# Feed-forwards with five plain units, residual sums kept in the matmul banks by ScalarE, normalised activations made by ScalarE and GpSimd, and gate sums ahead of a weight split

## The chip, the cores and the metric

The kernel runs on one core of a Trainium2 chip. A core has five engines that run their own instruction queues in order and meet through semaphores: TensorE (PE, matmuls; its weight loads are listed apart as PEld), VectorE (DVE), ScalarE (ACT), GpSimd (POOL) and SyncE (SP, which issues the transfers between the main memory and the on-chip memory SBUF). Matmul results go into banks of an accumulation memory (PSUM) of 128 partitions x 512 float32 each. The metric is the time on the device of one execution, in microseconds, as the median of several runs.

## The reference, cut to what matters

A decoder trunk of two layers, one sequence of 512 tokens, width 1024. The even layer's attention has two kinds of heads, the odd layer's forgets. Each layer adds an attention part and a gated feed-forward to x. The change lies in the feed-forward, and in a few lines of layer 1's attention.

```python
def conv_glu_ffn(h, w_in, conv_w, conv_b, w_out):
    a, b = jnp.split(h @ w_in, 2, axis=-1)              # 1024 -> 2 x 2816
    taps = conv_w[:, None, :]
    a = lax.conv_general_dilated(a, taps, window_strides=(1,), padding=[(CONV_WIDTH - 1, 0)],
                                 dimension_numbers=('NWC', 'WIO', 'NWC'),
                                 feature_group_count=a.shape[-1]) + conv_b
    return (jax.nn.silu(a) * b) @ w_out                 # 2816 -> 1024

def reference(x, ...):
    for layer in range(DEPTH):
        h = rmsnorm(x, attn_norm[layer])
        ...
        x = x + conv_glu_ffn(rmsnorm(x, ffn_norm[layer]), ffn_w_in[layer], ffn_conv_w[layer],
                             ffn_conv_b[layer], ffn_w_out[layer])
    return rmsnorm(x, final_norm)
```

In layer 1, `log_f = log_sigmoid(f + b_f)` is a gate for each head and token, and its running sum over the tokens goes into the attention scores.

## The kernel before, in words

**Layout.** Activations lie transposed, features on the partitions: `X[0..7]` are eight tiles of 128 features x 512 tokens. Every float32 matmul operand is split into a high and a low part (`whi`/`wlo` for weights, `xh`/`xl` for activations, `gh`/`gl` for the gated middle), and each product is three matmuls: high by high, low by high, high by low. ScalarE makes high parts (a cast), VectorE low parts (a subtraction).

**The plan.** From the attention on, work is written as jobs with an engine, a cost, what they depend on, a priority (smaller is sooner) and the buffers they take and give back (class `Plan`). `Plan.run` places the jobs by their costs, engine by engine, and the kernel issues the instructions in that order; each engine then runs its own in program order. So a cost or a priority in a call of `add` sets an order, not a time.

**A feed-forward** (`ffn`) has 22 units of 128 columns of `a` and 128 of `b`. Each unit is conv, silu, product, and gives `gh[c]`, `gl[c]`. Two kinds of units:

- *Plain* (`plain`, the first `PLAIN` = 6): two half units, each 8 x 3 matmuls of 512 columns into one of two banks (`mm`). The activation that enters is x times the norm's weight, without the root; VectorE multiplies the bank by `rstd` afterwards (`fa`, `fb`).
- *Seven products* (`seven`, the other 16): a 2 x 2 block scheme that needs seven block products in place of eight. Each product is 4 x 3 matmuls of 256 columns. It works on sums of weight blocks (`total` on VectorE, `cross` on GpSimd, tiles `sr`, `sp`, split into `sxh`, `sxl`) and on sums of normalised activation blocks. Those are made once, by `sums(k)` for k = 0 to 3, while the plain units run: two normalised tiles (`gh<-x,ng,rstd`), four sums of half a tile (tiles `d1`, `d3`, named `gl` in the trace), and their high and low parts in the tiles `b1`, `b2`, `t1`, `t3`. The results of a unit are put together from the banks `t`, `o` and four `f` banks.

`gate` and `gated` finish a unit: a scaled copy and a silu on ScalarE (tile `tt`), two taps of the convolution (`tap`), the product and the low part on VectorE.

**The output projection** is done in four parts (`PARTS`), after 6, 12, 17 and 22 units. `out(m, p)` multiplies part p's units into output tile m: its weights (`wo`) are loaded and split, each of its 5 or 6 units is a step of three matmuls into an `mm` bank, and VectorE adds the bank to `X[m]` (`x<-x,mm`). On TensorE a seven-product unit has priority 100 + c and a step of `out` 200 + p, so the steps fill the places where a unit isn't ready. In the last layer the fourth part is done token by token and goes straight into the final norm (`tokens`).

**Loads.** All weights are issued by SP in one chain: `wraw` (512 KB, two buffers) for plain units and for one half of a seven-product unit, `wb` (512 KB, two buffers) for its other half, `wo` for the output.

**Layer 1's gate sums.** At the start of layer 1's attention the kernel runs a queue of generators (`fl`): one unit, a group of values that also gives `lf` (the log of the gate), and three more units. `cums` then casts `lf` and multiplies it with a triangle of ones. The weights of the unit `U[1]` are split on VectorE at about the same place (line 91 is the helper through which every operation is recorded, so all rows of the profile have that line).

Of the kernel before, what the change touches and what calls it, by code (L numbers as in the profile page):

```python
# [18 lines left out]
P = 128  # L19
# [3 lines left out]
NF = 22  # L23
# [15 lines left out]
PARTS = ((0, 6), (6, 12), (12, 17), (17, 22))  # L39
PLAIN = 6  # L40
# [143 lines left out]
def trunk(ctx, tc, A):  # L184
# [112 lines left out]
    def unit(src, use, ps=None, hl=None):  # L297

        h, l = weights(src, [P, NK, P]) if hl is None else hl
# [108 lines left out]
    class Mixer:  # L408
# [11 lines left out]
        def weights(self, src, shape, place=None, token="w", split=None):  # L420
# [9 lines left out]
            def hi():  # L430
# [5 lines left out]
                              b, prio=p, give=("wraw",))  # L436
# [709 lines left out]
    def ffn(layer, nl, final):  # L1146
# [7 lines left out]
        with ExitStack() as es:  # L1154
# [3 lines left out]
            plan = Plan(dict(PE=0.0, ACT=2.6, DVE=2.6, POOL=4.9, SP=-5.0), dict(PE=0.03), wraw=2, wb=2, wo=2, w=2, mm=2, f=4, t=1, o=1,  # L1158
                        a=2, tt=1, b=2, g=10, sr=2, sp=1, slot=NK, sq=2)
            plan.bufs["w"], plan.bufs["slot"] = [], []  # L1160
            add = plan.add
            M = Mixer(plan, None, None)
            GH, GL, GJ = {}, {}, {}
            B = {n: [fp.tile([P, H, w], F32R, tag=f"{n}{x}", bufs=1, name=f"{n}{x}") for x in "hl"]
                 for n, w in (("b1", W), ("b2", SEQ), ("t1", SEQ), ("t3", SEQ))}

            MV = dict(b11=("b1", LO), b21=("b2", LO), b22=("b2", HI), t1=("t1", LO), t2=("t1", HI), t3=("t3", LO), t4=("t3", HI))
# [4 lines left out]

            def split(h, l, x, n, prio, *deps, take=(), give=()):

                j = add("ACT", 0.19 + 0.00085 * n, lambda: act.copy(h(), x()), *deps, prio=prio, take=take)
                return add("DVE", 0.16 + 0.00104 * n, lambda: dve.tensor_sub(l(), x(), h().bitcast(F32)), j, prio=prio, give=give)

            def gate(c, box, *deps):
# [12 lines left out]
                j = add("DVE", 0.72, lambda: tap(2), j, prio=p)  # L1191
                j = add("DVE", 0.72, lambda: tap(1), j, prio=p, give=("a",))
                return add("ACT", 0.68, lambda: silu.append(act.activation(box["t"], box["t"], AF.Silu).ins), j, prio=p)

            def gated(c, box, *deps):
# [7 lines left out]
                GJ[c] = add("DVE", 0.69, lambda: dve.tensor_sub(GL[c], box["b"], GH[c].bitcast(F32)), j, prio=p, give=("b",))  # L1203
# [27 lines left out]
            def plain(c, root):  # L1231
                box = {}
                ps = []
                for u in range(2):
                    w = M.weights(A["wfi"][layer, 2 * c + u], [P, NK, P]) if c else (dict(h=first[u][0], l=first[u][1]), None)
                    lastu = (c, u) == (PLAIN - 1, 1)
                    bx, j = {}, None
                    for k in range(NK):
                        def step(k=k, w=w, bx=bx):
                            if k == 0:  # L1240
                                bx["ps"] = mm_bank()
# [5 lines left out]
                        j = add("PE", 0.685, step, w[1], j, prio=100 + c, take=("mm",) if k == 0 else (), give=give)  # L1247
# [11 lines left out]
                j = add("DVE", 0.69, fa, ps[0][1], root[0], prio=1, take=("a",), give=("mm",))  # L1259
                t = gate(c, box, j)  # L1260
                j = add("DVE", 0.69, fb, ps[1][1], prio=1, take=("b",), give=("mm",))
# [3 lines left out]
            def sums(k, root):  # L1265

                x = {}

                def norm(c):
                    x[c] = g_tile("gh", F32)  # L1270
                    dve.scalar_tensor_tensor(x[c], X[c], ng[:, nl - 1, c:c + 1], rstd, op0=ALU.mult, op1=ALU.mult)
                    if c >= H:
                        x["d1"], x["d3"] = g_tile("gl", F32), g_tile("gl", F32)
                p = 2 + 0.1 * k
                j = add("DVE", 0.75, lambda: norm(k), root[0], prio=p, take=("g",))
                j = add("DVE", 0.75, lambda: norm(k + H), j, prio=p, take=("g",))
                eng, e, cost = (pool, "POOL", 0.74) if True else (dve, "DVE", 0.42)
                s1 = add(e, cost, lambda: eng.tensor_sub(x["d1"][:, LO], x[k][:, LO], x[k][:, HI]), j, prio=p)
                s2 = add(e, cost, lambda: eng.tensor_add(x["d1"][:, HI], x[k + H][:, HI], x["d1"][:, LO]), s1, prio=p)
                s3 = add(e, cost, lambda: eng.tensor_sub(x["d3"][:, LO], x[k + H][:, HI], x[k][:, HI]), s2, prio=p)  # L1280
                s4 = add(e, cost, lambda: eng.tensor_sub(x["d3"][:, HI], x["d1"][:, HI], x[k + H][:, LO]), s3, prio=p)
                part = lambda n, i: (lambda: B[n][i][:, k])
                a = split(part("b1", 0), part("b1", 1), lambda: x[k][:, LO], W, p, j, s4)
                b = split(part("b2", 0), part("b2", 1), lambda: x[k + H], SEQ, p, j, s4, give=("g",))
                c = split(part("t1", 0), part("t1", 1), lambda: x["d1"], SEQ, p, s2, s4)
                d = split(part("t3", 0), part("t3", 1), lambda: x["d3"], SEQ, p, s4, c, b, give=("g",))
                TJ.extend((a, b, c, d))

            order = [None] * 3
            count = [0]  # L1290

            def seven(c):

                w, box, sm, sj = [None] * 4, {}, {}, {}
                n0 = c * 0.001

                def load(u, pool_, tag):
# [555 lines left out]
```

## Time and profile before

| | |
|---|---|
| median of 3 runs | 1216.3 us (1215.74 to 1216.44) |
| the profiled execution | 1216.55 us |
| its span, first to last instruction | 1214.8 us |
| first feed-forward, first to last matmul of its own, about | 271 to 621 us |
| second feed-forward, about | 855 us to the end |
| granted TensorE clock | 0.999 |
| moved from the main memory | 119.80 MB, 100 GB/s over the span |

A row of a group reads: engine, operation, tiles written <- tiles read, shapes, count, then busy us and mean ns of one, then the engine's idle time just before and who ended it. A row of the order of time starts with the start and the duration in us. Matmuls overlap, so a matmul's duration (0.39 us for 512 columns) is longer than the distance from one start to the next; that distance is TensorE's pace. `mm<-xh,wlo` is a matmul of a plain unit, `mm<-gh,whi` one of `out`, and matmuls with `sxh` or `sxl` are those of seven-product units (named by their bank `f`, `t` or `o`).

### The profile page before, as it was taken

To read this page: it belongs to the slowest core of one execution; us is meant where nothing else is said; L and a number is where in the kernel's file an instruction comes from. 1 tells how busy PE (TensorE), PEld (TensorE's weight loads), DVE (VectorE), ACT (ScalarE), POOL (GpSimd) and SP (SyncE) were. 2 spreads that over 40 slices of the span, in tenths; PEclk is the share of its full clock that TensorE was granted. 3 is DMA by queue.
4 is the path that set the end of the run, shared out by engine and by line. 5 is a ranking of instruction groups with operands and counts; after the bars stand their busy time and mean duration, and the time that the engine had idled before them with its cause. 6 is when DMAs were issued, how large, how long until landed. Compare 5 with 4: busy or idle time off the path is not lost.

```text
span 1214.8 us, 19529 instructions
## 1 busy us (share of the span) xinstructions
PE 1205.3 (99%) x7491; PEld 1038.3 (85%) x7491; DVE 910.4 (75%) x1565; ACT 647.9 (53%) x1211; POOL 221.2 (18%) x262
## 2 busy tenths in 40 slices
PE   9999999999999999999999999999999999999998
PEld 6887877778898999999887878877889999999996
DVE  6867887679996898878774463446899779887883
ACT  6666577745554454444553664644555445454453
POOL 0000035423400100100121552411341000110100
PEclk9999999999999999999999999999999999999999
DMA  7322231122423223213224552322233223222331
GB/s 236 121 75 93 73 112 37 36 70 87 155 77 116 96 96 120 93 68 131 78 97 149 161 175 83 112 70 87 88 107 137 74 102 126 85 98 82 132 105 70
DMA packets 50685, 124.71 MB, mean 103 GB/s; under 512 B 6096, under 2 KB 16080, under 8 KB 50592
## 3 DMA queue, kind: packets, MB, share of 16 engines
q1 hardware_dynamic: 50304, 123.18, 30.3%
q8 instruction: 59, 0.97, 0.3%
q14 instruction: 34, 0.28, 0.1%
q10 hardware_dynamic: 288, 0.28, 0.1%
HBM read 119.80 MB, written 2.13 MB: 100 GB/s over the span
## 4 chain that ended last, share of the span: by engine, by line
PE 95%; DVE 2%; ACT 1%; issue 0%; POOL 0%; DMA 0%; DVEq 0%; SPq 0%; POOLq 0%; ACTq 0%
PE mm L91 55%; PE f L91 17%; PE t L91 12%; PE o L91 7%; PE s L91 4%; POOL e L91 0%; DMA x<-x 0%; DVE wlo L91 0%; ACT e L91 0%; DVE sxl L91 0%; DVE xl L91 0%; ACT whi L91 0%; DVE e L91 0%; DVE q L91 0%; ACT sq L91 0%
## 5 line engine op out<-in xcount | busy, mean ns | idle before, releaser
L91 PE MATMUL mm<-xh,whi 128*128 128x512 f32 x424 | 169.0, 399 | 0.0
L91 PE MATMUL mm<-xh,wlo 128*128 128x512 f32 x424 | 165.7, 391 | 0.0
L91 PE MATMUL mm<-xl,whi 128*128 128x512 f32 x424 | 165.3, 390 | 0.0
L91 DVE TENSOR_TENSOR wlo<-wraw,whi 128x1024 fp32r<-128x1024 f32 (+2 forms) x83 | 100.6, 1212 | 45.3 <-ACT whi L91 45.3
L91 POOL TENSOR_TENSOR sp<-wraw,wb 128x512 f32<-128x512 f32 x32 | 47.1, 1473 | 441.3 <-DMA wraw<-wfi 243.2
L91 PE MATMUL mm<-gh,wlo 128*128 128x512 f32 x312 | 122.1, 391 | 0.0
L91 PE MATMUL mm<-gh,whi 128*128 128x512 f32 x312 | 122.1, 391 | 0.0
L91 PE MATMUL mm<-gl,whi 128*128 128x512 f32 x312 | 121.4, 389 | 0.0
L91 ACT CAST whi<-wraw 128x1024 fp32r<-128x1024 f32 (+2 forms) x83 | 81.8, 985 | 65.3 <-PE mm L91 41.4
L91 DVE TENSOR_TENSOR x<-x,mm 128x512 f32<-128x512 f32 x96 | 65.4, 684 | 50.9 <-PE mm L91 50.5
L91 POOL TENSOR_SCALAR e<-e,dn 128x128 f32<-128x128 f32 (+3 forms) x128 | 76.5, 622 | 133.8 <-DVE dn L91 121.3
L91 PEld LDWEIGHTS mm<-xh,whi 128*128 128x128 f32 x424 | 79.8, 188 | 19.4 <-issue 3.7
L91 DVE SCALAR_TENSOR_TENSOR tt<-a,conv,tt 128x510 f32<-128x510 f32 x88 | 72.1, 819 | 31.5 <-ACT tt L91 30.7
L91 PEld LDWEIGHTS mm<-xh,wlo 128*128 128x128 f32 x424 | 79.8, 188 | 17.2 <-DVE wlo L91 1.9
L91 PEld LDWEIGHTS mm<-xl,whi 128*128 128x128 f32 x424 | 79.6, 188 | 16.8
L91 ACT CAST sxh<-sr 128x512 fp32r<-128x512 f32 x96 | 56.4, 617 | 68.1 <-DVE sr L91 68.1
L91 ACT ACTIVATE e<-e,nm 128x256 f32<-128x256 f32 (+3 forms) x128 | 70.8, 556 | 31.0 <-DVE nm L91 30.8
L91 ACT COPY a<-f 128x256 f32<-128x256 f32 x64 | 23.9, 373 | 112.6 <-PE f L91 111.7
L91 ACT CAST whi<-wo 128x768 fp32r<-128x768 f32 (+1 forms) x56 | 44.0, 789 | 54.4 <-PE mm L91 48.5
L91 PE MATMUL f<-t3l,sxh 128*128 128x256 f32 x256 | 72.4, 283 | 0.0
L91 PE MATMUL f<-t3h,sxl 128*128 128x256 f32 x256 | 72.4, 283 | 0.0
L91 PE MATMUL f<-t3h,sxh 128*128 128x256 f32 x256 | 72.4, 283 | 0.0
(311 smaller groups left out, 3496.1 us busy)
## 6 DMA issues: line engine op xcount, KB each, us to landing
wraw<-wfi SPq DMA_DIRECT2D x56, 512.0 KB
wb<-wfi SPq DMA_DIRECT2D x32, 512.0 KB
wraw<-wu SPq DMA_DIRECT2D x30, 512.0 KB
wo<-wfo SPq DMA_DIRECT2D x32, 384.0 KB
wraw<-wo SPq DMA_DIRECT2D x16, 512.0 KB
wo<-wfo SPq DMA_DIRECT2D x24, 320.0 KB
wraw<-wv SPq DMA_DIRECT2D x10, 512.0 KB
x<-x SPq DMA_DIRECT2D x16, 256.0 KB
```

Source lines behind the costliest of these rows:

```text
L91: r = f(*a, **k)
```

## The change

1. `PARTS` becomes ((0, 5), (5, 11), (11, 17), (17, 22)) and `PLAIN` 5: unit 5 is a seven-product unit, and the first output part has five units.
2. `sums(k)` is rewritten. ScalarE makes x times the norm's weight, GpSimd multiplies by `rstd`, in place, and makes the sums: one instruction of 128x512 for two differences, two of 128x256. All seven blocks of a k lie side by side, so that one cast (128x1792) and one low part (128x1792) do for all. The even k work in a tile `sx`, the odd ones in the tile `WB`, which is both buffers of the wide weights `wb`; the first wide load waits for the last low part. The priorities move these jobs among the plain units' splits.
3. `out(m, p)`, except for the first two tiles of the first part and for the part that feeds the next layer, starts from a bank into which ScalarE has copied `X[m]`, and ScalarE copies the bank back at the end; VectorE's addition goes.
4. On TensorE, units and output tiles have one common order (`at`), and a table of counts places the units between the tiles (`HOLD`). The last step of the first output tile is done after most of the second tile.
5. The low parts of plain units' weights get priority 1.05 (were 1.2), those of the first two output tiles too; some costs change.
6. In layer 1 the split of `U[1]`'s weights is issued behind the instruction that makes `lf`, and the gate sums come one step earlier.

The core of the diff:

```diff
-PARTS = ((0, 6), (6, 12), (12, 17), (17, 22))
-PLAIN = 6
+PARTS = ((0, 5), (5, 11), (11, 17), (17, 22))
+HOLD = 2
+PLAIN = 5
...
             c = self.plan.add("DVE", 0.16 + 0.00104 * n, lambda: dve.tensor_sub(box["l"], box["w"], box["h"].bitcast(F32)),
-                              b, prio=p, give=("wraw",))
+                              b, prio=p if low is None else low, give=("wraw",))
...
-                j = add("DVE", 0.72, lambda: tap(2), j, prio=p)
+                j = add("DVE", 1.0 if c < PLAIN else 0.77, lambda: tap(2), j, prio=p)
...
             def sums(k, root):
...
+                def weighted(c):
+                    out, src, _ = halves(c)
+                    act.activation(out, src, AF.Copy, scale=ng[:, nl - 1, c:c + 1])
+
+                def rooted(c):
+                    out, _, r = halves(c)
+                    pool.tensor_mul(out, out, r)
+                p = 1.2 + 0.0001 * (25,45,65,85)[k]
+                own = ("sx",) if n == 0 else ("wb", "wb")
+                if k in range(4):
+                    a = add("ACT", 0.62, lambda: weighted(k), prio=p, take=own)
+                    b = add("ACT", 0.62, lambda: weighted(k + H), a, prio=p)
+                    j = add("POOL", 1.9, lambda: rooted(k), a, root[0], prio=p)
+                    j = add("POOL", 1.9, lambda: rooted(k + H), b, j, prio=p)
...
+                j = add("POOL", 1.48, lambda: pool.tensor_sub(two(4, 6), two(1, 3), hi.unsqueeze(1).to_broadcast([P, 2, W])), j, prio=p)
+                j = add("POOL", 1.1, lambda: pool.tensor_add(e1, hi2, d1), j, prio=p)
+                j = add("POOL", 1.1, lambda: pool.tensor_sub(e3, e1, lo2), j, prio=p, lat=3.0)
+                j = add("ACT", 0.19 + 0.00085 * NC, lambda: act.copy(BX[0][:, k], x[:, W:]), j, prio=p + 0.004)
+                TJ.append(add("DVE", 2.6, lambda: dve.tensor_sub(BX[1][:, k], x[:, W:], BX[0][:, k].bitcast(F32)), j, prio=p + 0.004,
+                              give=("sx",) if n == 0 else ("wb", "wb")))
...
+                def wide_load(j):
+                    return add("SP", 0.35, load(1, "wb"), j, TJ[-1], prio=1 + n0, take=("wb",), lat=3.3)
...
+                if c == PLAIN:
+                    la = raw_load(M.prev_load)
+                    lb = M.prev_load = wide_load(la)
+                else:
+                    lb = wide_load(M.prev_load)
+                    la = M.prev_load = raw_load(lb)
...
+                onto = (use is None or final) and (p > 0 or m > 1)
+
+                def place():
+                    bx["ps"] = M.bank("mm")
+                    if onto:
+                        act.copy(bx["ps"], X[m])
+                if onto:
+                    bx["job"] = pl[0] = add("ACT", 0.62, place, XO.get(m), pl[0], gone[-2], prio=q, take=("b",))
...
+                def end():
+                    if onto:
+                        j = XO[m] = add("ACT", 0.62, lambda: act.copy(X[m], bx["ps"]), fo[0], prio=1, give=(bx["job"],))
+                    else:
+                        j = XO[m] = add("DVE", 0.69, lambda: dve.tensor_add(X[m], X[m], bx["ps"]), fo[0], XO.get(m), prio=1, give=(bx["job"],))
...
             for p in range(1, len(PARTS)):
-                c0, c1 = PARTS[p - 1]
-                sevens(range(done, c1))
-                done = max(done, c1)
+                own = list(range(max(PLAIN, PARTS[p][0]), PARTS[p][1]))
+                n, late, ready = len(own), HOLD if p == 1 else 1, None
                 for m in range(NK):
-                    if m % 2 == 0 and done < min(PARTS[p][1], c1 + 4):
-                        seven(done)
-                        done += 1
-                    out(m, p - 1, keep if final and p == len(PARTS) - 1 else None)
-            sevens(range(done, NF))
+                    while m >= late and (n - len(own)) * (NK - late) < (m - late + 1) * n:
+                        seven(own.pop(0))
+                    ready = out(m, p - 1, keep if final and p == len(PARTS) - 1 else None, ready)
+                sevens(own)
...
-                        dve.tensor_sub(lf[:, tb], y, ab)
+                        lfi[0] = dve.tensor_sub(lf[:, tb], y, ab).ins
...
-                   unit(U[1], q_use(1)), unit(U[9], k_use(1)))
+                   unit(U[1], q_use(1), behind=lfi), unit(U[9], k_use(1)))
...
-            fl.step(4)
+            fl.step(3)
```

More of the change, by code (lines that the diff above doesn't have):

```diff
@@ L295, in weights, with unit @@
         return h, l
-    def unit(src, use, ps=None, hl=None):
-        h, l = weights(src, [P, NK, P]) if hl is None else hl
+    def unit(src, use, ps=None, hl=None, behind=(None,)):
+        h, l = weights(src, [P, NK, P], behind=behind[0]) if hl is None else hl
         yield
@@ L418, in bank, with weights @@
             return bank([i for k, i in (job or self.plan.now).got if k == "b"][n], name)
-        def weights(self, src, shape, place=None, token="w", split=None):
+        def weights(self, src, shape, place=None, token="w", split=None, low=None):
             box, n, self.seq = {}, shape[1] * shape[2], self.seq + 1
@@ L1234, in plain @@
                 for u in range(2):
-                    w = M.weights(A["wfi"][layer, 2 * c + u], [P, NK, P]) if c else (dict(h=first[u][0], l=first[u][1]), None)
+                    w = M.weights(A["wfi"][layer, 2 * c + u], [P, NK, P], low=1.05) if c else (dict(h=first[u][0], l=first[u][1]), None)
                     lastu = (c, u) == (PLAIN - 1, 1)
@@ L1274, in sums @@
[L1274 to L1279, printed above, removed]
@@ L1286, in sums @@
-                d = split(part("t3", 0), part("t3", 1), lambda: x["d3"], SEQ, p, s4, c, b, give=("g",))
-                TJ.extend((a, b, c, d))
+                    out = x[:, SEQ:2 * SEQ] if c >= H else x[:, 0:SEQ].rearrange("p (h w) -> p h w", h=2)[:, ::-1]
+                    src, r = X[c], rstd
+                    if c < H:
+                        src, r = [t.rearrange("p (h w) -> p h w", h=2) for t in (X[c], rstd)]
+                    dve.scalar_tensor_tensor(out, src, ng[:, nl - 1, c:c + 1], r, op0=ALU.mult, op1=ALU.mult)
@@ new lines, in sums @@
+                p = 1.2 + 0.0001 * (25,45,65,85)[k]
[6 more added lines that the diff above has]
+                else:
+                    j = add("DVE", 0.82, lambda: norm(k), root[0], prio=p, take=own)
+                    j = add("DVE", 0.82, lambda: norm(k + H), j, prio=p)
@@ L1384, in seven, with out @@
                 gated(c, box, t, c21)
-            fo = [None]
-            def out(m, p, use=None):
+            fo, pl, XO, gone = [None], [None], {}, [None, None]
+            def out(m, p, use=None, ready=None):
                 c0, c1 = PARTS[p]
@@ new lines, in out, with steps, step @@
+                if onto:
+                    bx["job"] = pl[0] = add("ACT", 0.62, place, XO.get(m), pl[0], gone[-2], prio=q, take=("b",))
+                def steps(ks):
+                    for k in ks:
+                        def step(k=k):
+                            if k == 0 and not onto:
+                                place()
+                            h, l, gh, gl = w["h"][:, k], w["l"][:, k], GH[c0 + k], GL[c0 + k]
+                            mm(bx["ps"], h, gh, k == 0 and not onto, False, onto)
+                            mm(bx["ps"], l, gh, False, False, onto)
+                            mm(bx["ps"], h, gl, False, k == n - 1, onto)
+                        give = (("w",) if k == n - 1 else ()) + (("g",) * n if (k, m) == (n - 1, NK - 1) else ())
+                        fo[0] = add("PE", 0.685, step, wj, fo[0], bx.get("job") if k == 0 else None, GJ[c0 + k], prio=100 + at,
+                                    take=("b",) if k == 0 and not onto else (), give=give)
+                        bx.setdefault("job", fo[0])
@@ L1421, in sevens @@
+                if (m, p) == (0, 0):
+                    return steps, end, n - 1
+                if (m, p) == (1, 0):
+                    ready[0]([ready[2]])
+                    ready[1]()
+                steps([n - 1])
+                end()
             def sevens(cs):
@@ L1497, in product @@
                     w = cols.stop - cols.start
-                    j = add("PE", 0.45 * w / SEQ, turn, end, fo[0], *(xj[m] for m in range(4 * h, 4 * h + 4)), prio=210, take=own)
+                    j = add("PE", 0.45 * w / SEQ, turn, end, fo[0], *(xj[m] for m in range(4 * h, 4 * h + 4)), prio=310, take=own)
                     for k in range(c1 - c0):
```

121 lines of the change are left out of this document (61 added, 60 removed).

## The prediction

> **What bounds the kernel now.** I read the page's busy shares and chain first, then the busy time by stretches, then the order of time around each pause of TensorE.
>
> ```profile
> span 1214.8 us, 19529 instructions
> ...
> PE 1205.3 (99%) x7491; PEld 1038.3 (85%) x7491; DVE 910.4 (75%) x1565; ACT 647.9 (53%) x1211; POOL 221.2 (18%) x262
> ```
> ```profile
> PE 95%; DVE 2%; ACT 1%; issue 0%; POOL 0%; DMA 0%; DVEq 0%; SPq 0%; POOLq 0%; ACTq 0%
> ```
>
> TensorE is busy all the time and carries 95% of the chain. Time can go in two ways only: fewer or cheaper matmuls, or pauses closed. The busy share hides short pauses, so I take TensorE's pace from starts and counts.
>
> ```profile
> 278.00:310.00 32.00, 32.00 (x143) 26.40 (x142) 30.30 (x39) 17.32 (x26) 11.18 (x9) 1.00 0.30 99
> 408.10:419.40 11.30, 11.30 (x96) 11.30 (x95) 9.10 (x18) 5.07 (x10) 1.68 (x1) 1.00 0.31 98
> 282.30:338.00 55.70, 55.70 (x245) 45.50 (x244) 54.14 (x71) 31.43 (x48) 21.46 (x17) 1.00 0.35 120
> 338.00:621.00 283.00, 282.49 (x1874) 260.54 (x1874) 232.11 (x375) 137.26 (x238) 29.84 (x22) 1.00 0.28 95
> ```
>
> (Columns: PE, PEld, DVE, ACT, POOL, clock, DMA share, GB/s.) Row 1 is plain units: less the ragged two, 141 matmuls of 512 columns in 32.0 us, 0.227 us each. Row 2 is seven-product units: 94 of 256 columns in 11.3 us, 0.120 us each, more than half of 0.227, with the weight loads busy throughout. Rows 3 and 4 are the plain stage and the rest of the first feed-forward: VectorE is full in the plain stage (54.1 of 55.7) and at 82% later; ScalarE has room in both.
>
> ```profile
> 310.38 0.39 PE L91 MATMUL mm<-xh,whi 128*128 128x512 f32 x1
> 310.66 0.50 PE L91 MATMUL mm<-xh,wlo 128*128 128x512 f32 x1
> 311.00 0.40 PE L91 MATMUL mm<-xl,whi 128*128 128x512 f32 x1
> ```
> ```profile
> 1098.22 1.29 POOL L91 TENSOR_TENSOR sp<-wraw,wb 128x512 f32<-128x512 f32 x1 [11.63 <-DMA wraw<-wfi]
> ```
> ```profile
> 1098.43 1.64 DVE L91 TENSOR_TENSOR sxl<-sr,sxh 128x512 fp32r<-128x512 f32 x1
> ```
> ```profile
> 1099.33 0.28 PE L91 MATMUL t<-b2h,sxh 128*128 128x256 f32 x1
> 1100.12 0.39 PE L91 MATMUL t<-b2h,sxl 128*128 128x256 f32 x1 [0.52 <-DVE sxl L91]
> ```
>
> The pauses: starts that are further apart than the pace. There are nine in the two feed-forwards; the first and the last are shown. Four are in plain units, on a weight's low part (310.38 to 311.00 is 0.62 for two steps of 0.227: 0.17 lost); they add up to 0.8 us. Five are in seven-product units, on the fourth product's low part (1099.33 to 1100.12 is 0.79 for a step of 0.120: 0.67 lost); with the steps behind them they add up to 2.35 us. So the pauses are worth 3.15 us in all, and no edit here can gain more than that, the matmuls that go, and a pause in layer 1 (below).
>
> These last fences also show the resource that decides this change. VectorE's subtraction of 128x512 takes 0.68 us alone and 1.64 here: it stands until GpSimd's addition is over.
>
> **The change part by part.**
>
> *Unit 5 becomes a seven-product unit.* It had 48 matmuls of 0.227 (10.9 us) and gets 84 of 0.120 (10.1): **-0.8 per feed-forward, -1.6 in all**, on TensorE itself.
>
> *The normalised activations and their sums, during the plain units.* Off VectorE: eight scalings; sixteen low parts become four of 1792 columns. On ScalarE: eight scalings and four wide casts for sixteen casts. On GpSimd: per k two products and a double difference of 128x512 and two sums of 128x256, where it had four of 128x256.
>
> ```profile
> L91 DVE TENSOR_TENSOR wlo<-wraw,whi 128x1024 fp32r<-128x1024 f32 x9 | 11.7, 1303 | 0.0
> L91 DVE SCALAR_TENSOR_TENSOR tt<-a,conv,tt 128x510 f32<-128x510 f32 x6 | 6.5, 1090 | 0.0
> L91 DVE SCALAR_TENSOR_TENSOR gh<-x,ng,rstd 128x512 f32<-128x512 f32 x8 | 6.4, 819 | 0.0
> L91 DVE SCALAR_TENSOR_TENSOR tt<-a,conv,tt 128x511 f32<-128x511 f32 x6 | 5.6, 930 | 0.2
> L91 DVE TENSOR_TENSOR a<-mm,rstd 128x512 f32<-128x512 f32 x6 | 4.1, 684 | 0.0
> ```
> ```profile
> L91 DVE TENSOR_TENSOR b1l<-gh,b1h 128x256 fp32r<-128x256 f32 x4 | 2.7, 687 | 0.0
> L91 DVE TENSOR_TENSOR t3l<-gl,t3h 128x512 fp32r<-128x512 f32 x4 | 2.7, 682 | 0.0
> ```
> ```profile
> L91 DVE TENSOR_TENSOR x<-x,mm 128x512 f32<-128x512 f32 x32 | 21.9, 685 | 18.7 <-PE mm L91 18.5
> ```
> ```profile
> L91 DVE SCALAR_TENSOR_TENSOR tt<-a,conv,tt 128x510 f32<-128x510 f32 x16 | 12.0, 748 | 16.0 <-ACT tt L91 15.9
> L91 DVE SCALAR_TENSOR_TENSOR tt<-a,conv,tt 128x511 f32<-128x511 f32 x16 | 11.9, 747 | 0.1
> ```
> ```profile
> L91 DVE TENSOR_TENSOR a<-b,o 128x256 f32<-128x256 f32 x16 | 6.7, 416 | 1.1 <-PE o L91 0.9
> ```
> ```profile
> L91 DVE TENSOR_TENSOR wlo<-wraw,whi 128x1024 fp32r<-128x1024 f32 x1 | 1.2, 1226 | 0.5 <-ACT whi L91 0.5
> ```
>
> The first two fences are VectorE's groups in the plain stage, the next four those of the stage behind it, where GpSimd is mostly idle. The same operation is dearer in the first: 6 x (1.090 - 0.748) + 6 x (0.930 - 0.747) for the taps, 4 x (0.687 - 0.416) for the 256-column parts, 9 x (1.303 - 1.226) for the weights: 4.9 us, and with eight scalings at 0.07 over a tap's 0.75, 5.5 us that VectorE stood. `a<-mm,rstd`, which has one operand in a bank, is not dearer (684).
>
> ```profile
> L91 POOL TENSOR_TENSOR gl<-gh x16: 737/1451/2379, 283.7 to 908.7; 128x256 f32<-128x256 f32 x16
> ```
> ```profile
> 303.62 2.37 DVE L91 SCALAR_TENSOR_TENSOR tt<-a,conv,tt 128x510 f32<-128x510 f32 x2
> ```
> ```profile
> 335.82 1.52 DVE L91 SCALAR_TENSOR_TENSOR tt<-a,conv,tt 128x510 f32<-128x510 f32 x2
> ```
>
> Alone, at 0.74 (the least of the row above) and the 1.3 of the addition at 1098.22, GpSimd's work was 16 x 0.74 + 1.30 = 13.1 us and becomes 12 x 1.30 + 8 x 0.74 = 21.5 (the new products and the double difference are not in the trace; I price them as the addition of that size). Low bound of what VectorE will stand: in proportion, 5.5 x 21.5 / 13.1 = 9.0 us. High bound: every GpSimd operation meets VectorE, a large one for 1.64 - 0.68 = 0.96, a small one for (2.37 - 1.52) / 2 = 0.43: 15.0 us. VectorE's own work falls by 5.9 (scalings) and by 1.6: the sixteen parts, four groups of 2.7 like the two shown, are 10.8 less 1.1 stood, four of 1792 are 4 x (0.68 + 1280 x 0.00105) = 8.1, with the slope from 512 to 1024 columns.
>
> Does TensorE feel it? Before, the splits of the eighth and the tenth half unit were late by 0.2 (the first pause above, and its like). Ahead of the tenth VectorE now loses six scalings (4.4), and, as the splits get a better due time, about 2.0 of taps and gating of unit 3 move behind it. So it may stand 5.5 + 6.4 = **11.9 us** before TensorE waits; above that each microsecond goes onto TensorE, in each feed-forward. 11.9 is the middle of 9.0 to 15.0. I take a value below it, because GpSimd's two products a k can start while VectorE reads banks or waits for ScalarE, and put half of the plain units' pauses as gone: **-0.4**. The far ends are -0.8 and +3.1 for each feed-forward.
>
> The Trainium skill, "SBUF — State Buffer", section "Who interferes with whom", says that a VectorE operation with two SBUF inputs and a GpSimd one that reads SBUF exclude each other for the whole instruction, while one with a single SBUF input is free. The trace agrees (1.64 against 0.68; 684 for `a<-mm,rstd`). By it alone GpSimd's 21.5 us would all be lost wherever VectorE always has such work: 9.6 over the 11.9 in each feed-forward.
>
> *The way into the first seven-product unit.* Its wide weights lie where odd sums lie, so their load is issued only behind the last low part.
>
> ```profile
> 325.65 0.33 SPq L91 DMA_DIRECT2D wraw<-wfi  x1
> ```
> ```profile
> 329.03 1.58 POOL L91 TENSOR_TENSOR sp<-wraw,wb 128x512 f32<-128x512 f32 x1 [1.66 <-DMA wraw<-wfi]
> ```
> ```profile
> 334.62 0.68 DVE L91 TENSOR_TENSOR t3l<-gl,t3h 128x512 fp32r<-128x512 f32 x1
> ```
> ```profile
> 338.06 0.28 PE L91 MATMUL f<-b1h,sxh 128*128 128x256 f32 x1
> ```
>
> The last low part ended at 335.3. Ahead of it lay 7.5 us that are now behind it (unit 4's gating, unit 5's first steps, two splits, two sums). 335.3 - 7.5 - 7.5 (its own work that goes) - 5.5 + 9.0 to 15.0 stood gives 324 to 330. Then 3.4 us to land (325.65 to 329.03), two sums of 0.68, a cast of 0.62, a low part of 0.68: 330 to 336. TensorE's cover: plain units to 338.1 - 10.9 = 327.2, ten steps of the first two output tiles (30 x 0.227 = 6.8), the first product (1.4): 335.4. The other loads in SP's queue wait behind this one; they feed later tiles. Cost nothing; 0.6 at the far end.
>
> *X through the banks.* 22 additions of 0.685 (15 us a feed-forward) leave VectorE; ScalarE gets 44 copies.
>
> ```profile
> L91 ACT CAST gh<-b 128x512 fp32r<-128x512 f32 x17 | 10.4, 620 | 9.0 <-DVE b L91 8.9
> ```
> ```profile
> L91 ACT COPY a<-f 128x256 f32<-128x256 f32 x64 | 23.9, 373 | 112.6 <-PE f L91 111.7
> ```
>
> None is in the trace at 128x512 with a bank; from 0.62 (between SBUF tiles) to 2 x 0.37 (out of a bank, half the size) I take 0.65, near the row of its size: 29 us more on 137 of 283. TensorE is bound there, so this gains only what it does to pauses. The two banks: store 0.65, fetch 0.65 and two hand-overs are 1.7 us, and the tile in the other bank takes 15 matmuls, 3.4 us: hidden. Without that cover it would be 1.7 a tile. A copy into a bank waits for the store of the tile two before; behind it in ScalarE's queue stand casts of output weights and of parts, which VectorE and then TensorE wait for. They are planned a unit (10 us) ahead, so a wait of a copy's length passes.
>
> *Order and the fourth product.* Its pauses come where GpSimd's addition starts just before VectorE's subtraction. A freer VectorE meets it less often, but seventeen units meet it anew. I take half: **-1.2** (0 to -2.35).
>
> *Layer 1.*
>
> ```profile
> 640.02 1.23 DVE L91 TENSOR_TENSOR wlo<-wraw,whi 128x1024 fp32r<-128x1024 f32 x1 [0.85 <-ACT whi L91]
> ```
> ```profile
> 641.44 0.17 DVE L91 TENSOR_TENSOR lf<-fy,fab 128x16 f32<-128x16 f32 x1
> ```
> ```profile
> 641.46 0.39 PE L91 MATMUL mm<-xh,whi 128*128 128x512 f32 x1
> 642.00 1.22 PE L91 MATMUL s<-uo,lfp 128*128 128x512 f32 x5
> ```
>
> The gate sums wait 0.31 us behind that split, which now goes behind `lf`: **-0.3** (0 to -0.4; the split is due one unit later, 24 x 0.227 = 5.4 us).
>
> Sum: -1.6 - 0.4 - 1.2 - 0.3 = **-3.5**, and 0.3 back for new hand-overs: -3.2. The profiled execution took 1216.55 us, 1.75 outside its span, 0.25 over the median of 1216.3; the sum is a difference, so from the median it gives **1213.1**.
>
> **The rivals.**
> - *GpSimd holds VectorE* (slower). Place: the splits of the eighth to tenth half units. It decides from 11.9 us stood; near the high bound, with the order worse than I assume, 3 to 5 us late in each feed-forward: 8 - 1.6 - 1.2 - 0.3 = +4.9, 1221.2. For: VectorE is full there. Against: it loses 7.5 us of its own. The Trainium skill's rule above is this rival.
> - *A wash.* The pauses move but stay: only the matmuls go, and 0.5 to 1 us comes back, at the wide load or the splits: 1215.5. For: the five pauses are meetings of two engines, which a new order shifts at will.
>
> **How the numbers follow.** Measured differences under 0.2% (2.4 us) can't be told from none: 1213.9 to 1218.7. Forecast 0.45 (1211.2 to 1213.9), the wash 0.28, GpSimd 0.27. All pauses closed gives 1216.3 - 1.6 - 3.15 - 0.4 = 1211.2, the low end; the high end takes in the rival at 1221.5. Faster 0.45, same 0.29, slower 0.26.
>
> **What would show it.** Right: TensorE's steps in the plain stage stay at 0.227 with under 0.3 us lost; VectorE stands under 12 us there; the first seven-product unit starts 36 matmuls behind the plain units without a pause. Wrong: a start-to-start gap of microseconds at `wlo` in half units 7 to 10, or at `sxl<-sr` in the first seven-product unit, with GpSimd's products beside it; or a pause at a tile's first matmul for ScalarE's copy.

## The result, and the profile after

| | before | after |
|---|---|---|
| median of 6 runs each | 1216.27 us (1215.2 to 1216.44) | 1223.77 us (1222.93 to 1226.19) |
| ratio | | 1.0066, 95% interval 1.0053 to 1.0079 |
| the profiled execution, its span | 1216.55, 1214.8 | 1222.93, 1221.1 |
| first feed-forward, first matmul to last output step | 348.9 | 351.8 |
| layer 1, from there to the second feed-forward | 235.2 | 235.9 |
| second feed-forward to the end | 359.2 | 362.2 |
| pauses of TensorE in the plain units, by feed-forward | 0.40, 0.42 | 5.44, 5.33 |
| pauses in the seven-product units | 1.28, 1.07 | 0, 0 |

The change makes the kernel slower by 0.5 to 0.8%. The forecast was 1213.1; what came is the rival "GpSimd holds VectorE", priced at 1221.2, and 2.3 us beyond the top of the range.

The page of the changed kernel: busy time by engine, the chain by engine, and one row of the costliest groups.

```profile
span 1221.1 us, 19755 instructions
...
PE 1204.5 (99%) x7563; PEld 1039.8 (85%) x7563; DVE 900.6 (74%) x1503; ACT 705.8 (58%) x1305; POOL 242.8 (20%) x272
...
PE 89%; DVE 6%; issue 2%; ACT 1%; DMA 1%; POOL 0%; SPq 0%; DVEq 0%; POOLq 0%; ACTq 0%
...
L92 PE MATMUL mm<-xh,wlo 128*128 128x512 f32 x392 | 153.9, 393 | 7.9 <-DVE wlo L92 7.9
```

TensorE's part of the chain falls from 95 to 89% and VectorE's rises from 2 to 6%, though VectorE is busy for 10 us less in all. Its busy share says nothing; the last row does. TensorE's wait for a plain unit's low part is now 7.9 us, eight pauses. (By starts, with the slower matmuls behind each, the ten are 10.8 us.)

One of the long ones in the order of time: TensorE, then VectorE, ScalarE and GpSimd.

```profile
318.28 0.39 PE L92 MATMUL mm<-xl,whi 128*128 128x512 f32 x1
318.51 0.39 PE L92 MATMUL mm<-xh,whi 128*128 128x512 f32 x1
321.29 0.50 PE L92 MATMUL mm<-xh,wlo 128*128 128x512 f32 x1 [2.39 <-DVE wlo L92]
```
```profile
313.03 1.78 DVE L92 TENSOR_TENSOR b<-b,tt 128x512 f32<-128x512 f32 x1
...
316.45 3.11 DVE L92 TENSOR_TENSOR bl<-sx,bh 128x1792 fp32r<-128x1792 f32 x1
319.48 1.75 DVE L92 TENSOR_TENSOR wlo<-wraw,whi 128x1024 fp32r<-128x1024 f32 x1
```
```profile
315.37 1.04 ACT L92 CAST whi<-wraw 128x1024 fp32r<-128x1024 f32 x1
```
```profile
312.21 3.77 POOL L92 TENSOR_TENSOR wb<-wb,rstd 128x512 f32<-128x512 f32 x2 [3.32 <-ACT wb L92]
316.06 5.76 POOL L92 TENSOR_TENSOR wb<-wb 128x512 f32<-128x512 f32 x3
```

The weight's high part was there at 316.4. Its low part starts at 319.48, behind a wide low part that takes 3.11 us (2.01 alone), itself behind a gating that takes 1.78 (0.68 alone), with GpSimd's new products and sums beside both; and it takes 1.75 itself (1.22 alone). TensorE wanted it at 318.7.

Where the 6.4 us of the span come from: 2.9 in the first feed-forward, 3.0 in the second, 0.7 in layer 1, less 0.2 ahead of them. In a feed-forward 5.0 more of plain pauses, less 1.2 of the pauses at the fourth products, less 0.8 of matmuls, is 3.0.

### The profile page after: what moved, and what is told of

Same layout as the page of the kernel before. It is cut to its first block, busy times and chain, and to the rows that moved or that the text cites. A ratio compares the mean times of both kernels' runs of the same rounds, so it can differ in the third digit from the quotient of the medians.

```text
span 1221.1 us, 19755 instructions
## 1 busy us (share of the span) xinstructions
PE 1204.5 (99%) x7563; PEld 1039.8 (85%) x7563; DVE 900.6 (74%) x1503; ACT 705.8 (58%) x1305; POOL 242.8 (20%) x272
## 4 chain that ended last, share of the span: by engine, by line
PE 89%; DVE 6%; issue 2%; ACT 1%; DMA 1%; POOL 0%; SPq 0%; DVEq 0%; POOLq 0%; ACTq 0%
PE mm L92 48%; PE f L92 18%; PE t L92 12%; PE o L92 8%; PE s L92 4%; DVE wlo L92 2%; DVE bl L92 1%; DVE b L92 1%; DVE tt L92 1%; ACT whi L92 0%; DMA wraw<-wv 0%; POOL e L92 0%; DMA x<-x 0%; ACT e L92 0%; DVE xl L92 0%
## 5 line engine op out<-in xcount | busy, mean ns | idle before, releaser
L92 PE MATMUL mm<-xh,wlo 128*128 128x512 f32 x392 | 153.9, 393 | 7.9 <-DVE wlo L92 7.9
L92 PE MATMUL mm<-xh,whi 128*128 128x512 f32 x392 | 156.4, 399 | 0.0
L92 PE MATMUL f<-bl,sxh 128*128 128x256 f32 x544 | 154.0, 283 | 0.0
L92 PE MATMUL f<-bh,sxl 128*128 128x256 f32 x544 | 153.9, 283 | 0.0
L92 PE MATMUL f<-bh,sxh 128*128 128x256 f32 x544 | 153.8, 283 | 0.0
L92 PE MATMUL mm<-xl,whi 128*128 128x512 f32 x392 | 153.0, 390 | 0.0
L92 PEld LDWEIGHTS f<-bh,sxh 128*128 128x128 f32 x544 | 104.3, 192 | 1.3
L92 PEld LDWEIGHTS f<-bh,sxl 128*128 128x128 f32 x544 | 104.3, 192 | 1.3
L92 PEld LDWEIGHTS f<-bl,sxh 128*128 128x128 f32 x544 | 104.3, 192 | 0.0
L92 DVE SCALAR_TENSOR_TENSOR tt<-a,conv,tt 128x510 f32<-128x510 f32 x88 | 78.7, 894 | 16.6 <-ACT tt L92 16.0
```

What stands on the lines that cost most here:

```text
L92: r = f(*a, **k)
```

## The experiments

"Stood" is worked out in the same way for every kernel: for each VectorE instruction of the plain stage, from the first `a<-mm,rstd` on, its duration less the shortest of its operation and shape in that run, summed. (This counts every group; for the kernel before it gives 7.3 us, where the prediction's sum over five groups gave 5.5.) The pauses are from TensorE's starts, in us.

| kernel | products by the root | stood, ff 0 | pauses plain / behind it, ff 0 | time |
|---|---|---|---|---|
| before | VectorE | 7.3 | 0.4 / 1.3 | 1216.3 |
| after | GpSimd, 8 | 13.2 | 5.4 / 0 | 1223.8 |
| e1 | VectorE | 5.7 | 0 / 5.7 | 1223.7 |
| e2 | left out | 3.7 | 4.0 / 0 | 1218.5 |
| e3, sums on VectorE too | VectorE | 1.3 | 0 / 8.2 | 1228.8 |
| e4, six plain units | GpSimd, 8 | 13.5 | 5.3 / 0 | 1225.7 |
| e5, splits first | GpSimd, 8 | 11.7 | 4.2 / 1.5 | 1225.8 |
| e6, places exchanged | VectorE | 5.7 | 0 / 0.8 | 1214.0 |
| e10, e6 and unread products | both | 11.3 | 2.4 / 5.2 | 1228.8 |
| e11, e6 with two sets back | GpSimd, 4 | 9.8 | 2.1 / 1.1 | 1219.0 |
| e12, e6 with six plain units | VectorE | 7.3 | 0 / 0 | 1213.1 |

(e2, e3, e4 and e10 were run once. The pauses of e1, e2 and e3 hold 1.6, 1.7 and 3.3 us of slow clock, see the last section.)

### VectorE normalises

```diff
-                if k in range(4):
+                if k in range(0):
```

> The changed kernel, but VectorE normalises (eight scalings of 0.75 us a feed-forward) and GpSimd's eight products of 128x512 are gone; the sums stay on GpSimd. Theory A (GpSimd's operations hold VectorE off the shared memory port): VectorE loses 8 x 0.96 = 7.7 us of standing and gains 6.0 of work, so the pauses of the plain units fall a little, from 5.3-5.4 us to 3-4.5 in each feed-forward, the time to 1219-1222. Theory B (VectorE has too much work of its own in the shorter stage, whoever stands): 6 us more work puts the pauses at 8 us or more, the time at 1228 or more.

1223.72 us, ratio 1.0065 (1.0048 to 1.0081): the same time with other pauses. VectorE stands 5.7 us in place of 13.2, and the pauses in the plain units are all gone, although it does eight scalings more. In their place TensorE waits at the first seven-product unit. TensorE's waits by what ended them, VectorE, and SP's queue:

```profile
PE t L92 <- ACT sxh L92: 6.7, 2, 3.4
```
```profile
330.25 2.03 DVE L92 TENSOR_TENSOR bl<-wb,bh 128x1792 fp32r<-128x1792 f32 x1
```
```profile
332.31 0.33 SPq L92 DMA_DIRECT2D wb<-wfi  x1
```

The last low part ends at 332.3, not at 326.7, and the wide load that waits for it goes out only then, 5.6 us later than in the changed kernel; TensorE waits 3.3 us in each feed-forward. So the pauses of the change have one cause and this run's another, which the next runs take apart.

### The product by the root left out

The kernel leaves the multiplication by `rstd` out of the normalised activations; GpSimd makes the sums alone.

```diff
-                    pool.tensor_mul(out, out, r)
+                    del out, r
```

> The changed kernel with the product by the root left out of the sums (the output is not the reference's), in the same program order on the other engines: GpSimd's eight products of 1.3 us are gone and nothing takes their place. Theory A: VectorE's standing in the plain stage falls from 13.2 us to about 5.5, and the pauses of the plain units from 5.4 us to under 1 in each feed-forward; span about 1212. Theory B and theory C (the order: a low part of 1792 columns stands right ahead of a split in VectorE's queue): the pauses stay at 4 us or more, since VectorE's own work and its order are the same.

1218.48 us. VectorE, ScalarE and TensorE run the same instructions in the same order as in the change, so the order of VectorE's work alone can't be the cause. None of the change's five pauses is left. There is one pause of 2.3 us a feed-forward, at another place, the third half unit's first matmul, which waits for its bank. By size alone, 4.0 would speak for the theory of the order; the places speak against it. Waits, and VectorE:

```profile
PE mm L92 <- DVE a L92: 4.3, 2, 2.2
```
```profile
280.83 1.23 DVE L92 TENSOR_TENSOR rs_u<-rstd 128x512 f32<-128x512 f32 x1
282.09 1.67 DVE L92 SCALAR_TENSOR_TENSOR rs_u<-rs_t,rs_u 128x512 f32<-128x512 f32 x1
```

Without the root to wait for, GpSimd's sums start at once and meet the root's own chain on VectorE, whose steps take 0.69 alone: 2.0 us stood there, ahead of the stretch that the table's 3.7 counts. The same holding, at a spot that has no slack at all.

### VectorE does the sums too

```diff
-                j = add("POOL", 1.48, lambda: pool.tensor_sub(two(4, 6), ...
+                j = add("DVE", 0.69, lambda: dve.tensor_sub(two(4, 6), ...
```

(beside the edit of e1, and the two sums of 256 columns likewise, with the taps' and wide low parts' costs as without GpSimd)

> VectorE does the normalised activations and also the four sums, so GpSimd has nothing to read in the plain units. Theory A (VectorE stands while GpSimd reads): VectorE's standing in the plain units falls from 13.2 us (5.7 with GpSimd's sums alone) to under 1 us, which pays for most of the 7 us of sums that it takes on; the plain units keep their pauses under 1 us, and what pause there is lies at the first seven-product unit, as where VectorE normalised and GpSimd summed. Rival (VectorE's amount of work decides): 7 us more work on VectorE bring back 3 us or more of pauses in the plain units.

1228.78 us, plain pauses 0: the amount of work on VectorE did not make them. The same groups in the plain stage, of after and then of this kernel:

```profile
L92 DVE TENSOR_TENSOR wlo<-wraw,whi 128x1024 fp32r<-128x1024 f32 x9 | 14.1, 1572 | 0.4 <-ACT whi L92 0.4
L92 DVE SCALAR_TENSOR_TENSOR tt<-a,conv,tt 128x510 f32<-128x510 f32 x5 | 7.0, 1405 | 0.0
```
```profile
L92 DVE TENSOR_TENSOR wlo<-wraw,whi 128x1024 fp32r<-128x1024 f32 x9 | 11.0, 1220 | 0.5 <-ACT whi L92 0.4
L92 DVE SCALAR_TENSOR_TENSOR tt<-a,conv,tt 128x510 f32<-128x510 f32 x5 | 3.7, 744 | 0.0
```
```profile
PE f L92 <- DVE sxl L92: 4.0, 2, 2.0
PE t L92 <- ACT sxh L92: 3.7, 2, 1.9
```

With GpSimd idle a weight's low part is back at 1.22 and a tap at 0.74. What does not fit is the way into the first seven-product unit (the last fence, this kernel's waits): the last low part now ends at 334.1, and everything behind it is late. The expectation named that place but not its size: 8.2 us a feed-forward, some 3 of it the slow clock of the last section.

### Place, amount or order

Six plain units and the old division, the products still on GpSimd:

```diff
-PARTS = ((0, 5), (5, 11), (11, 17), (17, 22))
-PLAIN = 5
+PARTS = ((0, 6), (6, 12), (12, 17), (17, 22))
+PLAIN = 6
```

> The changed kernel with six plain units and the old parts: 10.9 us more of plain stage for the same sums. Theory A as a matter of place (the sums' first 45 us are as crowded as before): the pauses stay at 4 to 5.5 us in each feed-forward, and the span grows by 1.6 us for the two plain units, to about 1222. Theory B (a budget over the whole stage): there is 4 us more room, the pauses fall to about 1, the span to about 1214.

1225.68 us; the pauses are 5.3 us in the first feed-forward at the same five splits. VectorE is idle for 5.4 us of that stage, against 2.9 in after. A pause does not come from a full stage; it comes where a split is held. (The span, 1223.9 us, is 1.9 over the one expected with these pauses; a stretch of slow clock in the second feed-forward is 1.7 of it.)

The splits ahead of the wide low parts (each wide low part made to wait for the low part of one half unit):

```diff
+            WJ = {}
...
+                    WJ[2 * c + u] = w[1]
...
+            for j, u in zip(TJ, (5, 7, 8, 9)):
+                j.deps.append(WJ[u])
```

> The changed kernel with the four wide low parts put behind the splits of half units 6, 8, 9 and 10 in VectorE's order; no work is added or taken away. Theory C (order): the pauses of the plain units fall from 5.4 us to about 1.5 in each feed-forward, as the two largest (1.3 and 2.7) each have a wide low part of 2 to 3 us ahead of the late split; time about 1216. Theory A: VectorE stands as long (13 us), so what the splits gain is paid later, at the first seven-product unit, whose wide weights wait for the last low part: 2 to 4 us in all in each feed-forward, time 1219-1222.

1225.79 us, ratio 1.0081 (1.0066 to 1.0096). The pauses go from 5.4 to 4.2 in the plain units of the first feed-forward, and 1.5 comes at the first seven-product unit. The order chooses who is late, not how late: the place is as theory A expected, the pauses (5.7 us in all) and the time are above what it gave.

### The two small edits

X added by VectorE again, the order of units and tiles as changed:

```diff
-                onto = (use is None or final) and (p > 0 or m > 1)
+                onto = False
```

> The changed kernel with X added to the banks by VectorE, as before, not put into them by ScalarE; order of the units as changed. Theory (that edit took the pauses at the fourth products, 1.28 and 1.07 us before, 0 after): pauses of 1 to 2.4 us come back among the seven-product units, 1225 to 1226. Rival (the order of the units and of their loads took them): none come back, 1223.8. The plain units' pauses stay at 5.4 and 5.3 us by both.

1225.51 us, ratio 1.0078 (1.0063 to 1.0093), which overlaps that of the change. The median lies where the theory put it, but its mechanism is not there: no pause came back, and the profiled executions have the same feed-forwards (351.9 and 362.2 us, against 351.8 and 362.2). So ScalarE's copies did not take the pauses at the fourth products. What did is the new order of units, tiles and loads; it is left by exclusion (the old division of the output has none either, see e4), and which part of it was not tried. The stretch behind the plain units, first of after, then of this kernel (busy us of PE, PEld, DVE, ACT, POOL):

```profile
332.00:620.00 288.00, 288.00 (x1943) 267.60 (x1942) 231.63 (x372) 165.90 (x293) 29.78 (x22) 1.00 0.29 99
```
```profile
332.00:620.00 288.00, 288.00 (x1943) 267.56 (x1942) 244.62 (x394) 144.44 (x249) 31.20 (x23) 1.00 0.29 100
```

13 us more on VectorE, 21 less on ScalarE, and TensorE is busy throughout in both.

The layer 1 edit taken back:

```diff
-                   unit(U[1], q_use(1), behind=lfi), unit(U[9], k_use(1)))
+                   unit(U[1], q_use(1)), unit(U[9], k_use(1)))
...
-            fl.step(3)
+            fl.step(4)
```

> The changed kernel with the layer 1 edit alone taken back (the second query unit's weights load no longer behind the gate's difference, four steps instead of three). Theory (the 0.6 us that layer 1 lost are that edit or its loads): 1223.1, the first query-key product of layer 1 again 36.6 us behind the last output tile. Rival (they are the values' weights, which SP issued 2.7 us later at the end of the first feed-forward): no change, 1223.8, that product 37.2 us behind the last output tile.

1224.55 us, ratio 1.0076 (1.0059 to 1.0092). The pause at the gate sums comes back (0.31 and 0.11), and the first query-key product stands 37.20 us behind the last output tile, against 37.17 with the edit and 36.56 before. So the edit is worth nothing, and the 0.6 is something else: the weights of the second half of the values. ScalarE's cast and TensorE, of after, and the cast of before:

```profile
627.44 1.10 ACT L92 CAST whi<-wraw 128x1088 fp32r<-128x1088 f32 x1 [1.45 <-DMA wraw<-wv]
```
```profile
629.68 0.45 PE L92 MATMUL s<-acch,fine 128*128 128x512 f32 x1
630.52 0.50 PE L92 MATMUL s<-accl,fine 128*128 128x512 f32 x1 [0.39 <-DVE accl L92]
```
```profile
623.36 1.10 ACT L91 CAST whi<-wraw 128x1088 fp32r<-128x1088 f32 x1
```

SP issued the load of `wv` at 622.68 and 619.97, 0.4 us ahead of the last output step in both kernels, but it had landed 4.8 us later in the one and at most 3.4 in the other. `accl` stands behind that weight's low part on VectorE. Both kernels with six plain units (e4 and e12) have 36.4 us; the profiled ones with five, 37.0 to 37.7. Why the load takes longer there was not found.

### The repair: VectorE normalises, and the wide load does not wait

The sums of odd k lay in the buffers of the wide weights, so the fourth set was the last to leave them. With the places exchanged it is the third.

```diff
-                if k in range(4):
+                if k in range(0):
...
-                n = k % 2
+                n = 1 - k % 2
...
-                    return add("SP", 0.35, load(1, "wb"), j, TJ[-1], ...
+                    return add("SP", 0.35, load(1, "wb"), j, TJ[2], ...
```

> VectorE normalises, and the two places of the sums are exchanged, so that the third set of sums, not the fourth, is the last to lie in the tile into which the first wide load of a seven-product unit goes; the load waits for the third low part alone. Theory D (the 3.5 us at the first seven-product unit, where VectorE normalised, are the wide load that was issued only behind the fourth low part): the load goes out some 6 us earlier, that pause and the 0.6 us behind it go in both feed-forwards, plain pauses stay at 0: 1214, between 1212 and 1216, so at the time of the kernel before or under it. Rival (the fourth low part itself is late, or VectorE has not the time for the first unit's sums either way): the pause stays at 2 us or more a feed-forward, 1219 or more.

1213.97 us, ratio to before 0.9983 (0.9974 to 0.9992), as expected, and 9.8 us under the change. The load goes out 8.4 us earlier than in e1, and a wait of 0.5 us in two is left there. SP, TensorE's waits, and the plain stage of after and of this kernel:

```profile
323.88 0.33 SPq L92 DMA_DIRECT2D wb<-wfi  x1
```
```profile
PE t L92 <- DVE sxl L92: 0.5, 2, 0.3
```
```profile
277.50:332.00 54.50, 50.49 (x217) 40.03 (x216) 50.88 (x44) 29.66 (x35) 31.83 (x21) 1.00 0.32 111
```
```profile
277.50:332.00 54.50, 54.50 (x241) 44.82 (x240) 51.32 (x57) 28.60 (x33) 21.62 (x13) 1.00 0.39 129
```

VectorE is busy as long in both (50.9 and 51.3), but in the second with 57 instructions in place of 44, and TensorE does 24 matmuls more. What the move to GpSimd took off VectorE, VectorE spent standing.

### GpSimd's products by themselves

e6 with eight products on GpSimd whose result nothing reads, VectorE's work unchanged:

```diff
...
+                for _ in range(2):
+                    add("POOL", 1.9, lambda: pool.tensor_mul(scr[0], X[k], rstd), j, prio=p + 0.01)
```

> The kernel with VectorE normalising and the places of the sums exchanged (plain pauses 0, VectorE stood 5.7 us a feed-forward), and beside it eight GpSimd products of X by the root into a tile that nothing reads: GpSimd does as much as in the change (some 32 us busy in the plain units), VectorE's own work stays. Theory A: GpSimd's reading alone makes VectorE stand 10 us or more and brings back 2 us or more of pauses a feed-forward in the plain units, or, where the products fall later, at the first seven-product unit: 1217 or more. Rival (the chain through ScalarE and GpSimd, or the order of VectorE's work, made the pauses): standing is up, pauses stay under 1.5 us, 1215 or less.

1228.76 us. VectorE, ScalarE and TensorE run the same instructions in the same order as in e6; the eight products are all that differs. GpSimd's products in the plain stage; a low part and an operation on a bank, of VectorE, in e6 and then in this kernel; and TensorE's waits:

```profile
L92 POOL TENSOR_TENSOR scr<-x,rstd 128x512 f32<-128x512 f32 x7 | 12.9, 1849 | 0.2
```
```profile
L92 DVE TENSOR_TENSOR gl<-b,gh 128x512 fp32r<-128x512 f32 x4 | 2.7, 683 | 0.0
L92 DVE TENSOR_TENSOR a<-mm,rstd 128x512 f32<-128x512 f32 x5 | 3.4, 683 | 0.0
```
```profile
L92 DVE TENSOR_TENSOR gl<-b,gh 128x512 fp32r<-128x512 f32 x4 | 4.9, 1232 | 0.0
L92 DVE TENSOR_TENSOR a<-mm,rstd 128x512 f32<-128x512 f32 x5 | 3.4, 682 | 0.0
```
```profile
PE mm L92 <- DVE wlo L92: 4.8, 8, 1.0
PE mm L92 <- DVE gl L92: 3.1, 2, 1.6
```

Nothing reads these products. In the plain units GpSimd's sums start when VectorE hands them over, as in e6, and ScalarE waits for GpSimd nowhere, so no chain through ScalarE and GpSimd can be the cause. The products cost 14.8 us. VectorE stands 11.3 us a feed-forward in place of 5.7, and 7.6 us of pauses come, where there were 0.8. The Trainium skill, "SBUF — State Buffer", section "Who interferes with whom", has VectorE with two SBUF inputs and GpSimd reading SBUF hold each other off for whole instructions; this run agrees (1.23 us on average for 0.68 where both operands lie in SBUF, 0.68 in both kernels where one lies in a bank). The products also write a tile, so the run does not tell GpSimd's reading from its writing.

### Half of the products

(against e6)

```diff
-                if k in range(0):
+                if k in range(2):
```

> Two of the four sets normalised by ScalarE and GpSimd, two by VectorE; places exchanged. Theory A, standing in proportion to GpSimd's products: VectorE stands 9 to 10 us a feed-forward, between 5.7 and 13.2; the plain pauses lie between 0 and 5.4, nearest 1 to 2.5 since the standing is under the 11.9 us that VectorE had to spare: 1216 to 1219. Rival (all or nothing, one wait for the slow last set): 0 or over 5.

1218.96 us, ratio 1.0024 (1.0015 to 1.0034); the standing, 9.8, is as expected, but its distribution is what teaches. Two of TensorE's waits in the plain units, of after and then of this kernel:

```profile
294.82 0.50 PE L92 MATMUL mm<-xh,wlo 128*128 128x512 f32 x1 [0.39 <-DVE wlo L92]
301.56 0.50 PE L92 MATMUL mm<-xh,wlo 128*128 128x512 f32 x1 [1.01 <-DVE wlo L92]
```
```profile
295.22 0.50 PE L92 MATMUL mm<-xh,wlo 128*128 128x512 f32 x1 [0.42 <-DVE wlo L92]
301.96 0.50 PE L92 MATMUL mm<-xh,wlo 128*128 128x512 f32 x1 [1.00 <-DVE wlo L92]
```

The first two sets are on GpSimd in both, VectorE had stood 2.1, 4.1 and 5.1 us in both when the splits that begin near 285.5, 293 and 300.5 us ended, and the first two pauses are the same. The other pauses of the plain units went with the other two sets. VectorE stood 9.8 us in all, under the 11.9 that the prediction allowed, and TensorE paused all the same.

### Six plain units, and the layer 1 edit, on the repaired kernel

```diff
-PLAIN = 5
+PLAIN = 6
```

(with the old `PARTS`)

> VectorE normalising and places exchanged, but six plain units and the old division of the output as before the change. Theory (a unit taken from plain to seven products saves 0.8 us a feed-forward): 1.6 us over the 1214.0 of the kernel with five, so 1215.6. Rival (what five units save is eaten by less cover for the first seven-product unit): 1214 or less.

1213.08 us, ratio 0.9977 (0.9967 to 0.9986): the fastest of all, and the rival was right. TensorE has the 95% of the chain again that it had before. Layer 1's start:

```profile
625.40 0.39 PE L92 MATMUL s<-acch,fine 128*128 128x512 f32 x1
625.64 0.39 PE L92 MATMUL s<-accl,fine 128*128 128x512 f32 x1
```

A feed-forward takes as long with six as with five (347.0 and 347.1 us, first matmul to last output step): the 0.8 us of matmuls are spent on the 0.8 of pauses that shorter cover leaves in e6. The 0.9 us between the two kernels is layer 1, where the wait for `accl` does not come.

> VectorE normalising, places exchanged and the layer 1 edit taken back. Theory (that edit moves nothing): 1214.0. Rival (it gains as forecast, 0.3 us): 1214.3. A difference as small can only be read from the start of layer 1: the first query-key product stands 37.2 to 37.4 us behind the last output tile by the first, over 37.5 by the second.

This is e6 with the layer 1 edit taken back by the same diff as above: 1214.02 us, ratio 0.9984 (0.9975 to 0.9994), the query-key product 37.44 us behind the last output tile, against 37.40 in e6. It moves nothing here either.

## Why the prediction was wrong

- **The step that failed is "Does TensorE feel it?"** It gave VectorE one account of 11.9 us for the tenth half unit's split, to be overdrawn once, at its end, and put the pauses of the plain units at -0.4 us; they grew by 10.0. Every split has a due time of its own, and the trace of before had them: the low part of the fifth half unit (first row below) ended at 293.4, 0.8 us ahead of the matmul that reads it, that of the sixth 0.9 us ahead, that of the eighth just in time.

```profile
291.69 1.75 DVE L91 TENSOR_TENSOR wlo<-wraw,whi 128x1024 fp32r<-128x1024 f32 x1
```

  In the changed kernel the first pause came at that fifth split, when VectorE had stood 4.1 us, and a pause that is taken is not undone by slack later: of its 13.2 us stood, 5.4 became pauses, in five pieces. The account would have given 0.2 us: counted alike, VectorE had stood 5.6 us at the tenth split before, which allows 12.0, and 12.2 after; and the tenth split had no pause. e11 shows the same with 9.8 us stood, under the account, and 2.1 us of pauses.
- **The bounds held, the choice did not.** The forecast of 9.0 to 15.0 us stood holds the 13.2 measured; with the table's 7.3 in place of the 5.5 the low bound would have been 12.0, as much as the account. I took a value under 11.9 because GpSimd's products would start while VectorE reads banks or waits. They start when the root is there or ScalarE hands them over, and run into whatever VectorE has next; of the work between two splits most has two operands in SBUF.
- **The price of a meeting was a little low.** The high bound had 0.96 us for a large GpSimd operation. The wide low part lost 3.11 - 2.01 = 1.10, the gating 1.78 - 0.68 = 1.10.
- **The rival** had the mechanism, the direction and the kind of place (the splits of the eighth to tenth half unit; the trace shows those of the fifth to the ninth). It priced the pauses at 4 us more a feed-forward; 5.0 came. It also counted 0.3 us of gain in layer 1, where 0.7 was lost, and only half of the pauses at the fourth products as gone.
- **Unit 5 as seven products**, -0.8 a feed-forward: TensorE's matmuls did get that much shorter (the first feed-forward takes 0.7 us less than in e4, which has the same pauses in it). That it is worth 1.6 in time is not shown: on the repaired kernel it was eaten by cover.
- **The way into the first seven-product unit**: right. The last low part ended at 326.7 (324 to 330 was forecast), with no pause. e1 shows how thin that was: 5.6 us later, and it costs more than 3 us a feed-forward.
- **X through the banks**, nothing: right (e8).
- **The fourth products' pauses**, -1.2: the sign was right, the size half; all of it went. By e8 it was not the copies; the order is left.
- **Layer 1**, -0.3: wrong. The pause at the gate sums was closed, but the time was lost again before the first query-key product, and a late load cost 0.6 beside it.

## What to carry to other kernels

Work moved from VectorE to GpSimd is not off VectorE where both read SBUF: count each GpSimd operation there as time that VectorE may stand, and compare that with VectorE's own price for the same work (here 0.75 us a scaling on VectorE, against 1.3 us or more for a product on GpSimd). Hold slack against the due time of each consumer, not against the end of the stage. And when a pause is closed, look for the load that was hidden behind it: in e1 the whole gain was held back by one transfer that waited for the last user of a shared buffer, and the choice of that user was free.

## What the runs showed of the hardware

GpSimd is held as well as VectorE. Its double difference of 128x512 in e6:

```profile
L92 POOL TENSOR_TENSOR wb<-wb 128x512 f32<-128x512 f32 x2 | 4.2, 2120 | 20.4 <-DVE wb L92 20.4
```

That is 2.1 us on average, the two of the row 1.29 and 2.95; and the unread products of e10 took 1.85 on average, where the first products of after took 1.30 each.

TensorE's clock fell to half for stretches behind some pauses, a second cost that the pause itself does not show. The granted clock is the third figure from the right in these rows: e1 around its pause of 3.5 us, e3 behind one of 2.1 us, and after behind one of 2.6 us.

```profile
337.00:340.30 3.30, 1.05 (x6) 0.85 (x7) 2.58 (x5) 2.06 (x4) 0.00 (x0) 1.00 0.85 336
340.30:343.70 3.40, 3.40 (x18) 3.40 (x17) 2.49 (x4) 2.41 (x5) 1.48 (x1) 0.51 0.05 19
343.70:347.00 3.30, 3.30 (x27) 3.17 (x26) 2.81 (x6) 0.00 (x0) 0.00 (x0) 0.99 0.00 0
```
```profile
335.90:342.60 6.70, 4.63 (x18) 4.05 (x19) 4.41 (x6) 2.67 (x6) 1.54 (x1) 0.50 0.79 307
```
```profile
321.20:324.60 3.40, 3.31 (x14) 2.73 (x15) 3.40 (x5) 1.70 (x1) 0.62 (x1) 1.00 0.45 154
```

In e1's stretch of 3.4 us at half clock a matmul of 256 columns starts 0.21 us behind the one before it, and 0.12 us in the next row: by starts, 1.6 us lost. In the plain units of e2, e4 and e5 it is 1.7 to 1.8 a stretch. The Trainium skill, "TensorE: Matmul & The Clock Gate", Part 1, has the clock fall after at least one idle window of about 3.4 us. Here pauses of 2.1 to 2.8 us were enough in some places (both feed-forwards of e3, one of the two in e2, e4 and e5) and not in others (after). It is the likely reason why the runs of after spread over 3.3 us, at mean clocks of 0.996 to 0.999, and why their median lies 0.8 over the profiled one; a slower run of it was not profiled.
